# Expert search by fetched rows: indirect transfers of the chosen rows of both tables in place of dense products with all 16384 of them

## The chip, the cores and the metric

The program runs on one core of a Trainium2 chip as one launch. The metric is the device time of that launch in microseconds. TensorE is called PE here, VectorE DVE, ScalarE ACT, GpSimd POOL and SyncE SP, as in the profile.

## The reference, cut to what matters

Three blocks follow each other on 256 tokens of width 1024: a recurrent and attention block with a feed-forward part, a block with two kinds of attention and an expert search, and a block with long convolutions and 16 experts. The change touches the expert search of the second block and the vectors that modulate the second and third block.

```python
mod = jax.nn.silu(c) @ ada_w[l] + ada_b[l]             # six vectors; the third block has six more
...
def peer(h, wq, subkeys, u_tab, v_tab):                # h 256 x 1024; the tables 16384 x 1024
    q = (hf @ wq).reshape(T, PEER_HEADS, 2, PEER_DKEY // 2)
    sc = jnp.einsum('thpd,pnd->thpn', q, subkeys, preferred_element_type=jnp.float32)
    top_v, top_i = lax.top_k(sc, PEER_TOPK)            # 16 of 128, twice for each of 8 heads
    cand_v = (top_v[:, :, 0, :, None] + top_v[:, :, 1, None, :]).reshape(T, PEER_HEADS, -1)
    cand_id = (top_i[:, :, 0, :, None] * PEER_NKEYS + top_i[:, :, 1, None, :]).reshape(T, PEER_HEADS, -1)
    best_v, best_j = lax.top_k(cand_v, PEER_TOPK)      # 16 of 256 sums
    ids = jnp.take_along_axis(cand_id, best_j, axis=-1)
    ...                                                # g = softmax of best_v, by heads
    def block(args):
        xb, ib, gb = args
        ub = jnp.take(u_tab, ib, axis=0)
        a = jnp.einsum('td,ted->te', xb, ub, preferred_element_type=jnp.float32)
        w = gb * jax.nn.gelu(a, approximate=False)
        vb = jnp.take(v_tab, ib, axis=0)
        return jnp.einsum('te,ted->td', w.astype(vb.dtype), vb)
```

So each token has 8 x 16 = 128 chosen rows of either table.

## The kernel before

All weights come as one stream of 128 x 1024 pieces (512 KB) through a ring of five buffers that SP fills (K.start, K._load, L82 to L95). A product asks for its next piece by K.get (L114): ACT rounds the piece to an upper part whi (L108), DVE subtracts for a lower part wlo (L112), and up to three pieces are split ahead. A product of float32 accuracy is then three PE instructions (mm3, L155, with the lines L158 to L160). Some pieces of the stream are not taken by a product but consumed where they come: those of the modulation vectors (K.modulation, L329), eight pieces for each of twelve vectors. DVE multiplies such a piece by a column of silu(c) and adds it to a sum (L362 for the first, L364 for the others); four small products with ones and one DVE addition then make the vector (total, L343). The lists plan1 (L374), plan2 (L771) and plan3 (L1312) set the order of the stream: 32 of the 96 modulation pieces stand in the first block's feed-forward part, 8 in the second block's attention, 24 in the pass over the first table, 32 in the one over the second.

The function peer (L1028) is the expert search. Eight pairs of pieces of wq give the queries (L1064), four float32 products for each head give the scores of the half keys (L1072). What DVE does to choose runs as small background steps between the weights: top16 (L1082) on 128 scores twice and on 256 sums once, for 8 heads and 2 halves of the tokens, then gate (L1105) and decode (L1114). The chosen pairs go to DRAM by POOL's queue (pick_parts, L1142).

Nothing waits for the choice at first: the first table is multiplied whole. 128 pieces of peer_u give the products of all 16384 rows with all tokens, gelu of which fills A, four tiles of 32 KB a partition (gelu, L1170, over 64 pairs). Then the gates are spread over A: for four tokens at a time PE works out distances (L1198, L1199), ACT and DVE make one-hot operands of them (L1205, L1206), PE multiplies these (L1224) and DVE multiplies A by the result (L1231). No weights are used in that time. Then the second table is multiplied whole as well: 128 pieces of peer_v, each with 12 products of 128 x 128 by 128 x 512 (the loop after prep, L1249), into four banks, with the parts of A as the other operand (L268, L269).

From the middle of the second table's pass on, the spectra of the third block's filters are worked out in small steps between the weights (Spectra.steps, L1396); the products of the last three of eight pieces are held back until the second table is done, and lie beside the update of x (L1294, L1295) and the start of the third block (block3, whose first DVE addition is L1534). From there to the end nothing of the change is met again: the third block's products, and its 16 experts, whose weights come in pieces of 512 KB and of 1 MB (L1809).

Of the kernel before, what the change touches and what calls it, by code (L numbers as in the profile page):

```python
# [22 lines left out]
S = 256  # L23
# [4 lines left out]
# columns of the packed per-partition vectors: name -> (first column, count)  # L28
# [11 lines left out]
class K:  # L40
    """Pools, constants and the helpers that every part uses."""
# [4 lines left out]
    def __init__(self, ctx, tc, a):  # L46
# [14 lines left out]
        self.sums = None  # L61
# [35 lines left out]
    def _process(self, wait=False, lower=None):  # L97
        """Split the next item, or have it consumed; the lower part later, by what this returns, where wait is set."""
# [15 lines left out]
    def get(self):  # L114
        """The upper and the lower part of the next weights."""
# [13 lines left out]
    def ahead(self, n):  # L129
        """Have the parts of n weights ready; the look ahead goes on."""  # L130
# [4 lines left out]
    def drain_raw(self):  # L135
        """Consume the raw items that come next."""
# [25 lines left out]
    def cols_of(self, hT, out):  # L162
        """out [128 n, 256 t] = the next 1024 x 128 weights^T hT."""
# [4 lines left out]
    def pair(self, hT):  # L168
        """[128 n, 2, 256 t] of the next two tiles."""
# [5 lines left out]
    def rows_part(self, ps, hT, q, n=8):  # L175
        """Two banks [128 t, 512 n] (+)= a quarter of hT^T the next 256 x 512 weights, summed by n tiles."""
# [7 lines left out]
    def rows_of(self, hT, after=None):  # L184
        """Two banks [128 t, 512 n] = hT^T the next 1024 x 512 weights; after(q) follows each quarter of them."""
# [32 lines left out]
    def rms(self, pool, x, name, n=1024, junk=None):  # L218
        """1/rms of the rows of x [128, 2, n] -> [128, 2]."""
# [10 lines left out]
    def square(self, t, h, junk):  # L230
        """The sums of squares over half h of the rows t of x, for rms_x."""
# [2062 lines left out]
```

## Time and profile before

| what | us |
|---|---|
| device time, three runs without profile: median (lowest to highest) | 2697.01 (2696.55 to 2697.32) |
| span of the profiled execution, first to last instruction | 2692.9 |
| busy in it: PE, DVE, ACT, POOL | 2375.5, 1423.8, 881.2, 81.0 |
| its mean granted PE clock, of full speed | 0.924 |

The time of the profiled execution itself is not listed beside its span; the median of the other runs lies 4.1 us above the span. PE is busy for 88% of the span, but that is an average over stages: the profile's slices show PE at 9 tenths and more from the start to about 1700 us and at 7 tenths afterwards, with the DMA engines at 9 tenths and more from about 1800 us on. Stages are told apart by what runs in them: the first block to 462 us, the second block's attention to 623, the queries to 681, the first table to 1050, the gates to 1145, the second table to 1534, the third block to about 1750, the experts to the end.

### The profile page before, as it was taken

The numbers are of one execution on the slowest core, as the hardware profiler recorded it, in microseconds if no ns is written. First come the engines' busy times: TensorE is split into PE (matmuls) and PEld (weight loads), VectorE is DVE, ScalarE is ACT, GpSimd is POOL, SyncE is SP. The second block draws the span as 40 slices with busy tenths as digits, with TensorE's granted clock in tenths as the row PEclk, the third lists the DMA queues.
The fourth block names the chain that finished last, engine by engine and source line by source line (L and its number), as shares of the span: only waits on it lengthen the run. The fifth ranks groups of instructions, "written<-read, shape, count | busy, mean of one in ns | idle before, by whom it ended". The sixth has DMA issues, their size and how long they took to land.

```text
span 2692.9 us, 38200 instructions
## 1 busy us (share of the span) xinstructions
PE 2375.5 (88%) x15289; PEld 1722.5 (64%) x15289; DVE 1423.8 (53%) x2416; ACT 881.2 (33%) x1263; POOL 81.0 (3%) x65
## 2 busy tenths in 40 slices
PE   9999999999999999999999999787766666767676
PEld 8899998889999998777788899431211221211222
DVE  7876887767888866877777888610000000000001
ACT  5764544564444444444455544200000000000000
POOL 0100000000000000000000013100000000000000
PEclk9999999999999999999999999788777878877787
DMA  6555787744566775078855634899999999999997
GB/s 218 166 158 170 250 283 244 233 136 136 174 185 182 244 262 171 4 245 284 290 172 172 180 118 163 327 357 415 414 416 416 414 416 415 414 414 415 416 414 306
DMA packets 189481, 727.75 MB, mean 270 GB/s; under 512 B 31258, under 2 KB 36471, under 8 KB 165239
## 3 DMA queue, kind: packets, MB, share of 16 engines
q1 hardware_dynamic: 176086, 712.72, 72.5%
q10 hardware_dynamic: 13120, 12.32, 1.5%
q8 instruction: 120, 1.97, 0.3%
q14 instruction: 59, 0.48, 0.1%
q0 software_dynamic: 96, 0.26, 0.0%
HBM read 723.88 MB, written 1.36 MB: 269 GB/s over the span
## 4 chain that ended last, share of the span: by engine, by line
PE 62%; DMA 30%; DVE 5%; ACT 1%; issue 1%; POOL 0%; SPq 0%; POOLq 0%; ACTq 0%; DVEq 0%
DMA K<-in_moe_w_dram 14%; PE mm L158 11%; PE mm L160 11%; PE mm L159 11%; DMA we<-in_moe_w_dram 10%; DMA wraw<-in_moe_w_dram 5%; PE ac L158 5%; PE ac L160 5%; PE ac L159 5%; PE gated L1224 3%; PE mm L1973 1%; PE mm L2034 1%; DVE wlo L112 1%; PE mm L1930 1%; PE dist L1198 1%
## 5 line engine op out<-in xcount | busy, mean ns | idle before, releaser
L112 DVE TENSOR_TENSOR wlo<-wraw,whi 128x1024 fp32r<-128x1024 f32 x479 | 586.9, 1228 | 281.6 <-ACT whi L108 278.7
L108 ACT ACTIVATE whi<-wraw 128x1024 fp32r<-128x1024 f32 x484 | 510.9, 1059 | 562.7 <-PE mm L159 241.1
L158 PE MATMUL mm<-hT3h,whi 128*128 128x256 f32 x1152 | 327.6, 284 | 0.0
L1932 DVE TENSOR_TENSOR xe<-mm,m 128x256 f32<-128x256 f32 x15 | 6.4, 425 | 606.6 <-PE mm L1930 606.6
L159 PE MATMUL mm<-hT3l,whi 128*128 128x256 f32 x1152 | 326.7, 284 | 0.0
L160 PE MATMUL mm<-hT3h,wlo 128*128 128x256 f32 x1152 | 326.4, 283 | 0.0
L158 PEld LDWEIGHTS mm<-hT3h,whi 128*128 128x128 f32 x1152 | 221.6, 192 | 1.3 <-issue 1.2
L1973 PE MATMUL mm<-K,xe 128*32 128x512 f32 x864 | 150.3, 680 | 81.7 <-DMA K<-in_moe_w_dram 81.7
L159 PEld LDWEIGHTS mm<-hT3l,whi 128*128 128x128 f32 x1152 | 221.5, 192 | 0.4 <-DVE hT3l L316 0.4
L160 PEld LDWEIGHTS mm<-hT3h,wlo 128*128 128x128 f32 x1152 | 221.5, 192 | 0.0
L1973 PE MATMUL mm<-we,xe 128*32 128x512 f32 x864 | 148.3, 781 | 82.0 <-DMA we<-in_moe_w_dram 81.6
L158 PE MATMUL ac<-whi,Wh 128*128 128x512 f32 x512 | 204.9, 400 | 0.0
L160 PE MATMUL ac<-whi,Wl 128*128 128x512 f32 x512 | 202.2, 395 | 0.1
L159 PE MATMUL ac<-wlo,Wh 128*128 128x512 f32 x512 | 202.0, 394 | 0.0
L158 PE MATMUL mm<-hTh,whi 128*128 128x256 f32 x608 | 171.4, 282 | 0.8 <-DVE hTl L301 0.8
L160 PE MATMUL mm<-hTh,wlo 128*128 128x256 f32 x608 | 169.3, 278 | 2.8 <-DVE wlo L112 2.8
L159 PE MATMUL mm<-hTl,whi 128*128 128x256 f32 x608 | 168.9, 278 | 0.0
L1973 PEld LDWEIGHTS mm<-K,xe 128*32 128x32 f32 x864 | 22.1, 114 | 201.8 <-DMA K<-in_moe_w_dram 188.0
L1973 PEld LDWEIGHTS mm<-we,xe 128*32 128x32 f32 x864 | 21.0, 121 | 201.5 <-DMA we<-in_moe_w_dram 180.4
L2013 ACT ACTIVATE he<-mm 128x512 f32<-128x512 f32 x16 | 9.5, 596 | 417.7 <-PE mm L1973 417.7
L2022 ACT ACTIVATE heT<-mm 128x512 f32<-128x512 f32 x16 | 9.6, 597 | 383.2 <-PE mm L2020 383.2
L2040 DVE TENSOR_TENSOR ye<-mm,m 128x512 f32<-128x512 f32 x16 | 11.1, 692 | 212.9 <-PE mm L2034 212.9
(535 smaller groups left out, 4578.0 us busy)
## 6 DMA issues: line engine op xcount, KB each, us to landing
we<-in_moe_w_dram SPq DMA_DIRECT2D x160, 1024.0 KB
K<-in_moe_w_dram SPq DMA_DIRECT2D x122, 1024.0 KB
wraw<-in_peer_u_dram SPq DMA_DIRECT2D x128, 512.0 KB
wraw<-in_peer_v_dram SPq DMA_DIRECT2D x128, 512.0 KB
wraw<-in_moe_w_dram SPq DMA_DIRECT2D x100, 512.0 KB
K<-in_moe_w_dram SPq DMA_DIRECT2D x84, 512.0 KB
wraw<-in_w_in_dram SPq DMA_DIRECT2D x48, 512.0 KB
wraw<-in_ada_w_dram SPq DMA_DIRECT2D x48, 512.0 KB
```

The costliest lines, as they stand in the source:

```text
L108: nc.scalar.activation(hi, raw, AF.Copy)
L112: (lower or nc.vector).tensor_sub(lo, raw, hi)
L158: nc.tensor.matmul(out, lhs[0], rhs[0], start=start, stop=False)
L159: nc.tensor.matmul(out, lhs[0], rhs[1], start=False, stop=False)
L160: nc.tensor.matmul(out, lhs[1], rhs[0], start=False, stop=stop)
L1198: nc.tensor.matmul(p, z[0:14], mv[0:14], start=True, stop=True)
L1224: nc.tensor.matmul(p[:, g % 2 * 4 + i], o[0][:, i], o[1][:, i], start=True, stop=True)
L1930: nc.tensor.matmul(p[:, c], hl[:, t, c * 128:c * 128 + 128], oh[:, t, e], start=t == 0, stop=t == 1)
L1973: nc.tensor.matmul(p[32 * j:32 * j + 32], xe[:, c], w[j], start=c == 0, stop=c == 7)
L2022: nc.scalar.activation(heT, p, AF.Copy)
L2034: nc.tensor.matmul(p[32 * g:32 * g + 32], heT[:, o:o + 32], w[2 * fh + dh], start=q == 0, stop=q == 7)
L2040: nc.vector.tensor_mul(ye, p, m5)
```

## The change

The two dense passes, the one-hot products and the round trip of the chosen pairs through DRAM are gone. The tables are laid side by side in DRAM as one table uv of 16384 rows of 8 KB, a row of peer_u and the same row of peer_v behind it. A list s is one head for one half of the tokens (16 lists, 16 choices each); a choice e of a list is one item n = 16 s + e, and an item is one indirect transfer from POOL's queue that brings 128 rows, one for each token of the half, each to its token's partition: 128 x 2048 numbers, 1 MB. There are 256 items.

For each item DVE multiplies the u half of the rows by the tokens' h2 (held in PSUM, tokens on the partitions) and sums along the row (dot); ACT takes gelu of two sums at a time; DVE makes a diagonal matrix of the result times the gate (weigh); PE multiplies the v half of the rows by that diagonal, two float32 products of 128 x 128 by 128 x 512, and sums over the items in PSUM (add). Items go two by two in batches; the diagonals and products of a batch are issued in the next one, between its two dots. A place of 1 MB is freed by an item's products and refilled at once. There are 12 places at first, 17 from the end of the queries' products on, when the split buffers are given up, and 9 after batch 52, when two tiles are closed for the third block's filters.

Choosing is cut into 13 DVE steps for each list: the first list is chosen whole before the first transfer, three steps go before each of the six batches that lie between the queries' products, two after each of the others. The filters' spectra go one step a batch from about batch 58 on (the 67 steps come in two halves, the second from about batch 97 on, two steps a batch), and none of their products is held back. All 96 modulation pieces now stand in the first two blocks: 40 before the feed-forward part, 40 in it, 16 in the second block's attention.

```diff
         def use(s, ch):
             def f(raw):
                 if ch == 0:
-                    assert state.get("s", s) == s
-                    state["a"] = self.sums.tile([128, 1024], F32, name="mod_a", bufs=1)
-                    state["b"] = self.sums.tile([128, 256], F32, name="mod_b", bufs=1)
+                    if len(state) == self.sums_bufs:
+                        total(s - len(state))
+                    state[s] = [self.sums.tile([128, n], F32, name=f"mod_{n}", bufs=self.sums_bufs)
...
+def spread(weights, raw, first=0):
+    p, n, m = [], 0, len(weights) - first
+    for i, z in enumerate(weights):
+        p.append((z, None))
+        while i >= first and n < len(raw) * (i - first + 1) // m:
+            p.append(raw[n])
+            n += 1
...
+    return spread(p, early, 6) + spread(f, late, 8)
...
-    m = mod3 + late
-    for j in range(128):
-        p.append((a['peer_u'][j], None))
...
-    for j in range(128):
-        p.append((a['peer_v'][:, j], None))
...
+    return spread(p, raw, 2) + [(z, None) for z in o]
...
+    def refill():
+        while places and st['n'] < N and (st['n'] // 16 in ids):
+            owner, z = places.pop(0)
...
+            i = ids[n // 16]
+            nc.gpsimd.indirect_dma_start(out=z, out_offset=None, in_=a['uv'], in_offset=bass.IndirectOffsetOnAxis(ap=i[:, n % 16:n % 16 + 1], axis=0))
...
+    def dot(n):
+        u = rows[n][1][:, 0:1024]
+        nc.vector.scalar_tensor_tensor(u, u, 1.0, h2[0], op0=ALU.mult, op1=ALU.mult, accum_out=dots[s][:, e:e + 1])
...
+    def gelu(n):
+        nc.scalar.activation(acts[s][:, e:e + 2], dots[s][:, e:e + 2], AF.Gelu)
...
+    def weigh():
+        for n in pend:
+            d = tk.tile([128, 128], F32, name='diag', bufs=4)
+            nc.vector.tensor_scalar(d, k.ident, acts[s][:, e:e + 1], gates[s][:, e:e + 1], op0=ALU.mult, op1=ALU.mult)
...
+    def add(r):
+        for n, d in r:
+            for j in range(2):
+                nc.tensor.matmul(ys[0][:, 512 * j:512 * j + 512], d, rows[n][1][:, 1024 + 512 * j:1536 + 512 * j], start=n % 128 == 0, stop=n % 128 == 127)
+            release(n)
+        refill()
...
+    def batch(b):
+        n = 2 * b
+        dot(n)
+        r = weigh()
+        dot(n + 1)
+        gelu(n)
+        add(r)
+        if b == 64:
+            finish(0)
+        pend[:] = [n, n + 1]
...
     for r in range(8):
         k.later(half_scores, r, k.pair(hT))
+        if r == 1:
+            pump(99, 0)
+            refill()
+        if r >= 2:
+            pump(3, 1)
+            batch(nb)
+            nb += 1
+            refill()
...
-    for j2 in range(64):
-        k.later(gelu, j2, k.pair(hT))
...
+    for b in range(nb, N // 2):
+        if b == 64:
+            tokens(1)
+        batch(b)
+        pump(2, st['n'] // 16 + 3)
+        refill()
+        if b == 52:
+            closed.update(('E0', 'G0'))
...
+        for _ in range(1 if b < 96 else 2):
+            k.settle()
+            if steps:
+                steps.pop(0)()
```

Three places show what the engines are given. On DVE, in the stretch where the chosen indices are worked out, the order before is this (wlo are the lower parts of the first table's pieces, early is the tile that holds the scores and lists):

```order
L112 TENSOR_TENSOR wlo<-wraw,whi 128x1024
L1125 TENSOR_TENSOR early<-early,iota_6514 128x512
L1129 TENSOR_TENSOR early<-early 128x512
L1130 TENSOR_REDUCE early<-early 128x32
L112 TENSOR_TENSOR wlo<-wraw,whi 128x1024 x2
```

And this is a piece of the order now, a batch and the first half of the next (rowsL and rowsS are places, h is h2, dots the sums, diag the diagonals):

```order
L1200 SCALAR_TENSOR_TENSOR rowsL,dots<-rowsL,h_6944 128x1024
L1090 MAX early<-early 128x8
L1091 MAX_INDEX early<-early 128x8
L1093 MATCH_REPLACE early<-early 128x128
L1090 MAX early<-early 128x8
L1091 MAX_INDEX early<-early 128x8
L1200 SCALAR_TENSOR_TENSOR rowsL,dots<-rowsL,h_6944 128x1024
L1216 TENSOR_SCALAR diag<-ident,acts,gate 128x128 x2
L1200 SCALAR_TENSOR_TENSOR rowsS,dots<-rowsS,h_6944 128x1024
```

The lower parts of weights are gone from DVE; two dots and two diagonals a batch take their place, and the steps of choosing stand behind the batch's second dot, so that a dot that waits for its rows holds them up.

On PE, this is the order before at the end of the first table and the start of the gates (hT3 are the parts of h2, pk the chosen pairs):

```order
L158 MATMUL mm<-hT3h,whi 128x256
L159 MATMUL mm<-hT3l,whi 128x256
L160 MATMUL mm<-hT3h,wlo 128x256
L1198 LDWEIGHTS pk_7245
L1198 MATMUL dist_11625<-ohm,pk_7245 128x512
```

And now, in the later part of the fetched rows, where the filters' spectra run beside them (ys is the sum over the items, KR the transform's matrix and the filters' parts):

```order
L1226 MATMUL ys<-G_6765,diag 128x512 x2
L1226 MATMUL ys<-rowsL,diag 128x512 x4
L1226 MATMUL ys<-rowsS,diag 128x512 x2
L158 MATMUL mm<-KR 128x256
L159 MATMUL mm<-KR 128x256
L160 MATMUL mm<-KR 128x256
```

PE's long runs of products with weights become four float32 products a batch, and each spectrum step's products wait behind the batch's.

On POOL's queue this stood in the same part of the program before:

```order
L112 TENSOR_TENSOR wlo<-wraw,whi 128x1024
L1152 MEMSET pk_7245 37x512
L1142 DMA picks<-early 128x4x128 x2
L1211 MEMSET pk_11618 37x512
L1525 MEMSET px_router 128x256
```

And now (early, G and G are the first twelve places):

```order
L112 TENSOR_TENSOR wlo<-wraw,whi 128x1024
L1174 DMA early_6762<-in_uv_dram,ids 128x2048 x3
L1174 DMA G_6763<-in_uv_dram,ids 128x2048 x4
L1174 DMA G_6765<-in_uv_dram,ids 128x2048 x4
L1174 DMA early_6762<-in_uv_dram,ids 128x2048 x4
L1174 DMA G_6763<-in_uv_dram,ids 128x2048 x4
```

POOL, which issued two transfers in the whole program, issues 256, in the order of the items, each waiting for its place and its list.

## Rows read from the trace of the kernel before

**Rows 1.** Stretches of the span, by stage: start and end in us, their length, then the busy us (and instructions) of PE, PEld, DVE, ACT and POOL, the granted PE clock, the DMA engines' share and GB/s.

```profile
0.00:275.00 275.00, 262.76 (x1807) 242.97 (x1808) 200.88 (x353) 158.02 (x249) 15.46 (x10) 0.99 0.57 176
275.00:462.00 187.00, 185.37 (x1340) 170.00 (x1339) 155.70 (x192) 87.38 (x100) 0.00 (x0) 1.00 0.81 273
462.00:623.00 161.00, 154.08 (x977) 131.44 (x975) 116.39 (x226) 88.97 (x188) 12.99 (x9) 0.97 0.53 168
623.00:681.00 58.00, 57.20 (x469) 56.67 (x469) 41.98 (x110) 29.58 (x49) 0.00 (x0) 0.98 0.51 152
681.00:1050.00 369.00, 369.00 (x3083) 367.11 (x3082) 288.95 (x546) 172.34 (x199) 1.91 (x3) 1.00 0.68 218
1050.00:1145.00 95.00, 93.74 (x649) 71.38 (x646) 83.15 (x191) 44.39 (x66) 0.35 (x1) 1.00 0.04 9
1145.00:1534.00 389.00, 388.94 (x1788) 312.63 (x1787) 296.91 (x340) 192.60 (x235) 0.00 (x0) 1.00 0.68 227
1750.00:2650.00 900.00, 646.02 (x3636) 187.98 (x3628) 55.14 (x103) 21.07 (x36) 0.00 (x0) 0.81 1.01 411
```

**Rows 2.** The chain that ended last, cut to 600 to 1760 us, shares by line.

```profile
by line: PE mm L160 15.0%; PE mm L158 14.9%; PE mm L159 14.9%; PE ac L158 10.4%; PE ac L160 10.3%; PE ac L159 10.2%; PE gated L1224 5.9%; PE dist L1198 1.7%; PE mm L1973 1.7%; issue 0.9%; PE mm L1429 0.7%; PE mm L1944 0.7%; PE mm L1072 0.6%
```

**Rows 3.** The timeline at the start of the queries and at the end of the second table: start and length in us, engine, line, operation.

```profile
622.67 0.58 PE L158 MATMUL mm<-hT3h,whi 128*128 128x256 f32 x1
...
1533.71 0.69 DVE L1294 TENSOR_TENSOR K<-ac,g 128x512 f32<-128x512 f32 x1 [1.66 <-PE ac L160]
1534.44 0.69 DVE L1295 TENSOR_TENSOR x<-x,K 128x512 f32<-128x512 f32 x1
...
1539.31 1.78 DVE L1534 TENSOR_TENSOR x<-x,K 128x512 f32<-128x512 f32 x1
```

**Rows 4.** DVE instructions of the forms that a batch will have, by their lines: count, shortest, median and longest in ns, first and last start.

```profile
L1538 DVE SCALAR_TENSOR_TENSOR x<-x,rsf,K x2: 1277/1281/1285, 1544.8 to 1546.2; 128x1024 f32<-128x1024 f32 x2
L1538 DVE DVE_READ_ACCUMULATOR x<-x,rsf,K x2: 82/83/84, 1546.0 to 1547.4; 128x1 f32 x2
L1119 DVE TENSOR_SCALAR early<-early x2: 220/220/221, 834.1 to 885.6; 128x128 uint32<-128x128 uint32 x2
```

**Rows 5.** Instructions on the tile early (the choice) from 626.5 to 1050 us, and on the tile K (the filters' spectra) from 1145 to 1534 us, columns as in rows 1.

```profile
626.50:1050.00 423.50, 8.91 (x66) 8.06 (x66) 136.67 (x474) 10.55 (x26) 1.74 (x2) 1.00 0.66 210
```
```profile
1145.00:1534.00 389.00, 13.87 (x80) 8.67 (x80) 72.64 (x111) 28.61 (x45) 0.00 (x0) 1.00 0.68 227
```

**Rows 6.** Float32 products on PE: by line as in rows 4, at 128 and at 512 columns, and one piece of the experts' timeline.

```profile
L1224 PE MATMUL gated<-oh,oh x512: 275/275/377, 1051.4 to 1143.9; 128*128 128x128 f32 x171
```
```profile
L1999 PE MATMUL ac<-x,ident x8: 592/1061/1061, 1771.1 to 1776.3; 128*128 128x512 f32 x8
```
```profile
1802.61 3.62 PE L1973 MATMUL mm<-we,xe 128*32 128x512 f32 x32
```

**Rows 7.** Transfers: two issue lines of the page, and two stretches as in rows 1.

```profile
we<-in_moe_w_dram SPq DMA_DIRECT2D x160, 1024.0 KB
wraw<-in_peer_u_dram SPq DMA_DIRECT2D x128, 512.0 KB
```
```profile
380.00:400.00 20.00, 20.00 (x147) 18.79 (x146) 17.70 (x24) 9.79 (x12) 0.00 (x0) 1.00 0.90 324
...
1800.00:2600.00 800.00, 566.29 (x3182) 158.84 (x3174) 40.98 (x78) 15.53 (x26) 0.00 (x0) 0.82 1.02 415
```

**Rows 8.** The transfers that POOL issues: their instruction as in rows 4, and the time from issue to landing in us.

```profile
L1142 POOL DMA_DIRECT2D picks<-early x2: 768/872/976, 878.3 to 931.2; - x2
...
DMA to landing us min/median/max: 4.3/4.6/4.9
```

**Rows 9.** The timeline where POOL computes beside DVE, and the same DVE form without POOL (by line, as in rows 4).

```profile
615.44 2.34 POOL L112 TENSOR_TENSOR wlo<-wraw,whi 128x1024 fp32r<-128x1024 f32 x1 [3.48 <-ACT whi L108]
615.53 3.91 DVE L1059 TENSOR_SCALAR early<-x,rsm 128x1024 f32<-128x1024 f32 x2
```
```profile
L834 DVE TENSOR_SCALAR on<-x,rsm x2: 748/748/749, 467.1 to 467.8; 128x1024 f32<-128x1024 f32 x2
```

**Rows 10.** The modulation sums on DVE by line, as in rows 4, and the three fullest stretches of DVE before the feed-forward part, as in rows 1.

```profile
L364 DVE SCALAR_TENSOR_TENSOR mod_a<-wraw,mod_t,mod_a x84: 1274/1279/1283, 279.8 to 1332.3; 128x1024 f32<-128x1024 f32 x84
```
```profile
20.00:40.00 20.00, 20.00 (x113) 17.40 (x112) 17.81 (x47) 10.62 (x15) 0.00 (x0) 1.00 0.62 193
100.00:120.00 20.00, 19.90 (x133) 17.93 (x131) 18.43 (x20) 17.66 (x24) 4.70 (x2) 1.00 0.54 169
120.00:140.00 20.00, 18.10 (x153) 17.57 (x154) 19.28 (x31) 10.18 (x14) 0.00 (x0) 1.00 0.52 154
```

More of the change, by code (lines that the diff above doesn't have):

```diff
@@ L279, in transposed, with full @@
         nc = self.nc
+        def full(n, c):
+            return tmp[n] if isinstance(tmp, list) else tmp[:, c]
         hi, lo = hT
@@ new lines, in peer, with pump, add_places, views @@
+    work = [(s, f) for s in range(16) for f in choose(s)]
+    def pump(n, upto):
+        while n and work and work[0][0] <= upto:
+            work.pop(0)[1]()
+            n -= 1
+    N = 256
+    places, rows, use = [], {}, {}
+    def add_places(owner, tiles):
+        use[owner] = 0
+        places.extend((owner, z) for z in tiles)
+    def views(tile):
+        return [tile[:, 2048 * i:2048 * i + 2048] for i in range(4)]
+    add_places("E0", views(E0)[1:])
+    add_places("G0", views(G0))
@@ new lines, in peer @@
+    add_places("G1", views(G1))
+    places.append(("E0", views(E0)[0]))
+    closed = set()
+    st = {"n": 0}
+    def refill():
+        while places and st["n"] < N and st["n"] // 16 in ids:
+            owner, z = places.pop(0)
+            if owner in closed:
+                continue
+            n = st["n"]
+            z = z() if callable(z) else z
+            rows[n] = owner, z
+            use[owner] += 1
+            i = ids[n // 16]
+            nc.gpsimd.indirect_dma_start(out=z, out_offset=None, in_=a["uv"],
+                                         in_offset=bass.IndirectOffsetOnAxis(ap=i[:, n % 16:n % 16 + 1], axis=0))
+            st["n"] += 1
@@ new lines, in release, with tokens @@
+    def release(n):
+        owner, z = rows.pop(n)
+        use[owner] -= 1
+        if owner not in closed:
+            places.append((owner, again.get(owner, z)))
+    again = {}
+    h2 = [None]
+    def tokens(t):
+        h2[0] = ps.tile([128, 1024], F32, name="h2")
+        for c in range(8):
+            nc.tensor.transpose(h2[0][:, c * 128:c * 128 + 128], hfull[:, c, t * 128:t * 128 + 128], k.ident)
+    dots, acts, pend = {}, {}, []
+    def dot(n):
+        s, e = n // 16, n % 16
+        if e == 0:
+            dots[s] = tk.tile([128, 16], F32, name="dots", bufs=3)
+        u = rows[n][1][:, 0:1024]
+        nc.vector.scalar_tensor_tensor(u, u, 1.0, h2[0], op0=ALU.mult, op1=ALU.mult, accum_out=dots[s][:, e:e + 1])
@@ L1210, in peer @@
[L1210 to L1234 removed]
+    assert not k.parts
@@ L1236, in peer @@
+    add(weigh())
+    k.settle()
+    while steps:
+        steps.pop(0)()
+        k.settle()
+    F.loads()
+    finish(1)
+    k.settle()
     ps.release()
+    pr.release()
+    pl.release()
+    tk.release()
     k.ps = tc.alloc_tile_pool(name="ps2", bufs=4, space=PSUM, reuse_waits="tile")
[L1238 to L1244 removed]
@@ L1389, in constant, with steps @@
         return [lambda i=i: self.k.parts_of(parts[0][:, i], parts[1][:, i], r[:, i]) for i in range(n)]
-    def space(self, pool):
-        self.room = [self.R[:, 7168:8192]] + [pool.tile([128, 1024], F32R, name=f"held{i}") for i in range(3)]
-        return pool
-    def steps(self):
+    def steps(self, o):
         k, N = self.k, 256
@@ L1417, in split @@
         def split(o, ch, s):
-            if o and ch in (1, 2):
-                z = self.room[2 * (ch - 1) + s]
-                return [z[:, 512 * i:512 * i + 512].rearrange("p (t c) -> p t c", t=2) for i in range(2)]
             b = 5120 + 1024 * s
@@ L1544, in block3 @@
     k.still = False
-    for f in F.held[4:]:
-        f()
     k.settle()
```

415 lines of the change are left out of this document (148 added, 267 removed).

## The prediction

> **What bounds the kernel now.** I read the stages first [rows 1]: a share of the whole span says little here, since the stages have different limits. Through both blocks and the whole expert search PE is the full engine: 369 of 369 us in the first table, 94 of 95 in the gates, 389 of 389 in the second table, at a granted clock of 1.00. DVE is second there with 76 to 88% and the DMA engines move 218 and 227 GB/s, and next to nothing during the gates. In the experts it is the other way round: the DMA engines are full at 411 GB/s and PE waits. The chain says the same of the stretch in question: the weights' products have three quarters of it, the gates' products 8% [rows 2]. So what is taken from PE between 681 and 1534 us is taken from the end, if nothing else fills that time; and the experts' stretch, which hangs on its own bytes, follows unchanged.
>
> The stretch that the change rewrites runs from the first product of the queries at 622.7 us to the first addition of the third block at 1539.3, when x is complete [rows 3]: 916.6 us.
>
> **What replaces it.** Four resources have to be priced for a batch of two items.
>
> *Fetching.* An item is 1 MB in rows of 8 KB. The nearest row is the experts' 1 MB pieces, which stream at 415 GB/s for 800 us [rows 7]: 1.049 MB / 415 = 2.53 us an item, 5.05 a batch. The 512 KB pieces of 4 KB rows give a second rate: 324 GB/s at a share of 0.90, so 360 when full, 2.91 us an item. Rows picked at random are like neither; I take the first, since size of transfer and of row are the same, and keep the second for the range. The Trainium skill (DMA: Bandwidth & Descriptors, Where 436 GB/s comes from) holds that a load from DRAM is bound by about 358 GB/s a core; by that figure an item would take 2.93 us and the sum below would end at 2593; the experts' 415 GB/s speak against it as a limit of this core.
>
> *DVE.* A dot is the form of L1538 with its accumulator read: 1.281 + 0.083 = 1.364 us; a diagonal is a 128-column tensor_scalar, 0.220 [rows 4]. Two of each make 3.17 us a batch. Choosing costs 136.7 us for 16 lists [rows 5], 8.5 a list; seven short instructions that served a half of the tokens are now issued for each list, so I take 9.5 a list, 1.46 for two of 13 steps. The spectra cost DVE 72.6 us [rows 5], 1.1 us for each of 67 steps.
>
> *PE.* A float32 product is two instructions in the rows (512 for 256 products on L1224). Their lengths, 275 ns at 128 columns and 592 at 512, differ by 0.83 ns a column, so 512 columns occupy PE for 0.42 us, and eight passes of four column groups take 3.62 us, 0.43 each [rows 6]. A batch is four products, eight passes: 3.45 us at full clock. At the lower of PE's two levels, 1.2 GHz, an instruction takes 1061 ns, 0.47 longer than at 2.4 GHz [rows 6], so about 0.86 to 0.9 a pass, 6.9 us or more a batch.
>
> *POOL.* An indirect transfer is in no row. Below stands the instruction of the plain transfers, 0.87 us for 512 pieces of 256 B; above, their 4.6 us from issue to landing, as if each transfer had to land before the next is begun [rows 8]. With eight or more places waiting I take it near the lower end, under 2.5 us, so that fetching sets the pace.
>
> Now the stages. **Queries with the first six batches:** 58 us as before [rows 1], plus the products of five batches, 5 x 3.45 = 17, plus eight transposes of h2, 2 us, plus 3 us in which DVE waits for the first rows (10 us of choosing, then a transfer of about 5, against three pieces split ahead): 80 us. The first list is chosen beside products that are under way. **Batches 6 to 57:** DVE 3.17 + 1.46 = 4.63, PE 3.45, fetching 5.05, which wins: 52 x 5.05 = 263. **Batches 58 to 96,** where a spectrum step joins the choice: DVE 3.17 + 1.46 + 1.10 = 5.73 is now above fetching; 39 x 5.73 = 224. **Batches 97 to 113,** choice done, two steps each: 3.17 + 2.20 = 5.37; 17 x 5.37 = 91. **Batches 114 to 127:** fetching, 14 x 5.05 = 71. The queue of filled places (12, later 9) lets fetching and DVE catch up with each other between these parts; against that gain stand the turn between the token halves at batch 64, where DVE waits for transposes and PE for the update of x, and late lists. I leave both out of the sum. **End:** the last four products 3.5 and the second half's update, four DVE instructions of 0.69 as L1294 and L1295 [rows 3], 2.8: 6. Sum 80 + 263 + 224 + 91 + 71 + 6 = 735 us against 916.6: **182 us less**.
>
> **The modulation pieces.** In the two tables they cost PE nothing, so taking 56 of them away gains nothing that is not counted. In the first two blocks each adds 1.28 us of DVE [rows 10]: 40 before the feed-forward part make 51 us on top of 201 in 275, eight more there 10 on 156 in 187, eight more in the attention 10 on 116 in 161 [rows 1]. On average PE covers it. Where DVE is fullest it does not: 3.9 us more for every 20 us puts 17.8, 18.4 and 19.3 at 21.7, 22.3 and 23.2 [rows 10], an excess of 7 us that PE waits for; with the order on DVE, where a piece stands ahead of the next weights' lower part, I take 12 us, from 0 to 35. The DMA share of 0.57 there has room for 21 MB.
>
> The third block's held-back products go, but they only lie beside a chain of DVE and ACT steps; I cost them at nothing, up to 5 us more or less. Nothing later changes, so a shift of the third block's start shifts the end.
>
> Sum: -182 + 12 = -170. The profiled span of 2692.9 becomes 2523; with the 4.1 us that the median of the runs lies above it, **2527 us**.
>
> **Rivals.**
>
> *Rows come more slowly than pieces.* For: they are scattered, and half-size pieces move at 360 GB/s. Against: every row is 8 KB. At 2.91 us an item a batch takes 5.82 in all four parts, 122 x 5.82 = 710 instead of 649: 2588 us.
>
> *POOL cannot issue fast enough, and the kernel gets slower.* Place: POOL's queue, where 234 transfers are still to be made ready after the queries. The gain of 170 is spent when a batch takes (649 + 170) / 122 = 6.71 us, 3.36 us an item; at 4.6 an item [rows 8] the batches take 1122 us and the kernel 3000. For: the program has no indirect transfer to show, and POOL and DVE get into each other's way in this trace: two DVE instructions of L1059 took 3.91 us together beside a POOL instruction of 2.34, where two of the same form on L834 take 0.75 each [rows 9], and DVE would be busy nearly without a break. Against: 512 pieces took POOL 0.87 us, an item has 128. The Trainium skill (SBUF — State Buffer, SBUF: two separate sides) has the rule that speaks against this change: POOL writes the descriptors of its transfers through a port pair that it shares with DVE, and a DVE instruction in a two-port mode shuts it out until it ends. By that rule the short diagonals and copies would hold POOL up, some 0.5 us a batch, and not the dots.
>
> *The clock.* In the experts PE is busy for 0.72 of the stretch, waits for each piece, and is granted 0.81 [rows 1]. If it stood at the lower level through all batches, 122 x 6.9 = 842 instead of 649: 2720 us, slower. Against: at that level PE would never wait, and the three stretches from 681 to 1534 us, in which PE hardly waits, are granted 1.00.
>
> *A full overlap.* If places in stock even out fetching and DVE, 234 items and some 6 MB of the filters' tables beside them take 606 us, and the blocks cover all their sums: 43 + 12 us less, 2472.
>
> **How the numbers follow.** Chances: forecast 0.50 (2490 to 2560), slower rows 0.24, POOL 0.15, the clock 0.03, full overlap 0.08. What a measurement of this kernel can tell from no change is 0.2%, 5 us. The range must hold 8 in 10: forecast, overlap and slower rows make 0.82, so it goes from 2470 to 2660, which is a batch of 6.3 us. Faster: 0.50 + 0.24 + 0.08, and a little of a mild POOL, 0.83; the same 0.02; slower 0.15.
>
> **What would show it.** Right: the stretch from the queries to the third block takes about 735 us; DMA at 0.95 and 400 GB/s or more in batches 6 to 57, then DVE above 0.95 with dots of 1.36 us; PE near 0.7 with a clock of 0.95 or more; POOL's instruction under 2.5 us; the first block longer by about 10 us and PE there waiting for wlo. Wrong: DVE waiting for rows while the DMA engines are not full (POOL), DMA full at 360 GB/s (slow rows), PE full at a clock near 0.5, or PE in the first block waiting for more than 35 us.

## The result: 118 us less, where 170 were forecast

| what | before | now |
|---|---|---|
| device time, median of the runs shown with this result (lowest to highest) | 2696.78 (2696.3 to 2697.32) | 2578.41 (2575.36 to 2579.39) |
| ratio, 95% interval | | 0.9556 (0.9543 to 0.957) |
| span of the profiled execution | 2692.9 | 2577.2 |
| its mean granted PE clock | 0.924 | 0.898 |

The forecast was 2527 us with a range of 2470 to 2660: the direction and the range held, and the time came out 51 us above the forecast. First the places that answer to [rows 3], from the timeline of the changed kernel: start and length in us, engine, line, operation.

```profile
651.77 0.58 PE L158 MATMUL mm<-hT3h,whi 128*128 128x256 f32 x1
...
1419.47 1.51 DVE L1531 TENSOR_TENSOR x<-x,K 128x512 f32<-128x512 f32 x1
```

The first product of the queries comes 29.1 us later than before (622.67), so the two first blocks lost that much. From there to the first DVE addition of the third block it now takes 767.7 us, against 916.6: 148.9 less. From that addition to the end it is 1157.7 us against 1153.6, 4.1 more. 29.1 - 148.9 + 4.1 = -115.7, which is the difference of the spans.

The stretch in between is cut at the starts of the dots that open batches 0, 6, 58, 97 and 114. These are the windows of the changed kernel as in [rows 1]: both first blocks; the queries with the first six batches; batches 6 to 57; 58 to 96; 97 to 113; 114 to 127; and the experts.

```profile
0.00:651.80 651.80, 614.21 (x4175) 548.59 (x4175) 537.89 (x831) 333.46 (x535) 29.40 (x18) 0.98 0.72 241
651.80:734.60 82.80, 68.10 (x431) 57.76 (x430) 54.39 (x131) 29.81 (x54) 20.23 (x20) 0.88 0.80 314
734.60:992.10 257.50, 206.07 (x485) 85.20 (x484) 219.06 (x602) 36.20 (x90) 98.53 (x105) 0.98 1.01 416
992.10:1212.90 220.80, 170.79 (x449) 77.68 (x449) 197.93 (x503) 41.61 (x90) 74.32 (x76) 0.92 0.96 381
1212.90:1345.70 132.80, 96.50 (x299) 49.41 (x297) 85.31 (x164) 18.48 (x45) 34.67 (x36) 0.86 0.85 326
1345.70:1410.90 65.20, 54.17 (x139) 24.39 (x140) 41.31 (x85) 4.14 (x17) 19.64 (x21) 0.97 0.87 349
1600.00:2500.00 900.00, 638.02 (x3568) 189.56 (x3564) 69.66 (x161) 23.53 (x41) 2.38 (x2) 0.81 1.00 406
```

| part | forecast, us | measured, us |
|---|---|---|
| first two blocks, more than before | 12 (0 to 35) | 29.1 |
| queries and first six batches | 80 | 82.8 |
| batches 6 to 57 | 263 | 257.5 |
| batches 58 to 96 | 224 | 220.8 |
| **batches 97 to 113** | **91** | **132.8** |
| batches 114 to 127 | 71 | 65.2 |
| end | 6 | 8.6 |
| third block to the end, more than before | 0 (-5 to 5) | 4.1 |

Two lines carry the error: 42 us in seventeen batches and 17 us in the first two blocks; the other lines give 5 us back in sum. That makes 54 us on the spans; it is 51 on the medians, since the median now lies 1.2 us above the profiled span and not 4.1. In batches 6 to 57 the DMA engines are full at 416 GB/s, as forecast. In 97 to 113 nothing is full: DMA 0.85, DVE 85 of 133 us, PE 97.

The instructions of a batch by their lines, as in [rows 4] and [rows 8]:

```profile
L1200 DVE SCALAR_TENSOR_TENSOR G<-G,h x120: 1200/1215/1223, 694.6 to 1409.6; 128x1024 f32<-128x1024 f32 x120
L1200 DVE DVE_READ_ACCUMULATOR G<-G,h x120: 70/83/85, 695.7 to 1410.8; 128x1 f32 x120
...
L1216 DVE TENSOR_SCALAR diag<-ident,acts,gate x256: 327/343/578, 694.1 to 1411.4; 128x128 f32<-128x128 f32 x128
...
L1174 POOL DMA_INDIRECT G<-in_uv_dram,ids x120: 935/939/1765, 679.5 to 1396.2; - x120
```

A dot takes 1.30 us (forecast 1.36), a diagonal 0.34 (0.22), an indirect transfer holds POOL for 0.94 (0.87 to 4.6). Now what DVE waited for in batches 97 to 113, and then what PE waited for: us in total, times, longest.

```profile
DVE KR L269 <- ACT KR L268: 17.8, 6, 7.1
DVE K L142 <- PE mm L1441: 17.3, 4, 4.5
DVE K L142 <- PE mm L1424: 5.9, 2, 3.7
DVE K L1433 <- ACT K L1430: 4.7, 4, 1.2
DVE rowsL L1200 <- DMA rowsL<-in_uv_dram,ids: 0.7, 1, 0.7
```
```profile
PE ys L1226 <- DVE diag L1216: 33.8, 11, 6.8
```

DVE's waits are 46 us, 2.7 a batch, and nearly all stand inside the spectrum steps; rows are waited for once. PE's 34 us are all for diagonals. A piece of the timeline there shows how they come about (in brackets the idle time ahead of an instruction, and what ended it):

```profile
1227.47 0.68 DVE L1436 TENSOR_TENSOR K<-K 128x512 f32<-128x512 f32 x1
1228.18 0.69 DVE L1437 TENSOR_TENSOR K<-K 128x512 f32<-128x512 f32 x1
...
1229.93 0.60 DVE L1216 TENSOR_SCALAR diag<-ident,acts,gate 128x128 f32<-128x128 f32 x2
1230.33 5.74 PE L1226 MATMUL ys<-rowsL,diag 128*128 128x512 f32 x8 [6.75 <-DVE diag L1216]
...
1238.05 0.59 PE L1441 MATMUL mm<-K,ones 128*128 128x256 f32 x2
...
1238.68 1.76 DVE L142 RECIPROCAL K<-mm 128x256 f32<-128x256 f32 x1 [4.22 <-PE mm L1441]
```

PE stands for 6.75 us until DVE, busy and waiting in a spectrum step (K), comes to the diagonals. Then PE has the items' products and a step's products first, the small product of L1441 comes last, and DVE stands for 4.22 us until it is there. In that time DVE makes no diagonals for the next batch. Each engine goes through its own queue in order, and each stands while the other has work for it further back.

### The profile page after: what moved, and what is told of

Same layout as the page of the kernel before. It is cut to its first block, busy times and chain, and to the rows that moved or that the text cites. A ratio compares the mean times of both kernels' runs of the same rounds, so it can differ in the third digit from the quotient of the medians.

```text
span 2577.2 us, 29437 instructions
## 1 busy us (share of the span) xinstructions
PE 2063.1 (80%) x11067; PEld 1200.5 (47%) x11067; DVE 1374.0 (53%) x2774; ACT 566.4 (22%) x998; POOL 326.8 (13%) x317
## 3 DMA queue, kind: packets, MB, share of 16 engines
q0 software_dynamic: 36864, 268.45, 25.8%
## 5 line engine op out<-in xcount | busy, mean ns | idle before, releaser
L112 DVE TENSOR_TENSOR wlo<-wraw,whi 128x1024 fp32r<-128x1024 f32 x223 | 276.2, 1242 | 95.9 <-ACT whi L108 94.1
L108 ACT ACTIVATE whi<-wraw 128x1024 fp32r<-128x1024 f32 x228 | 239.5, 1056 | 177.9 <-PE mm L159 53.1
L1226 PE MATMUL ys<-G,diag 128*128 128x512 f32 x480 | 228.9, 617 | 50.7 <-DVE diag L1216 50.5
L1200 DVE SCALAR_TENSOR_TENSOR G<-G,h 128x1024 f32<-128x1024 f32 x120 | 145.5, 1214 | 25.7 <-DMA G<-in_uv_dram,ids 25.3
L1226 PE MATMUL ys<-rowsS,diag 128*128 128x512 f32 x252 | 126.3, 641 | 36.3 <-DVE diag L1216 29.5
L1174 POOL DMA_INDIRECT G<-in_uv_dram,ids x120 | 115.4, 962 | 207.2 <-PE ys L1226 100.7
L1226 PE MATMUL ys<-rowsL,diag 128*128 128x512 f32 x168 | 96.5, 716 | 49.0 <-DVE diag L1216 48.6
L158 PEld LDWEIGHTS mm<-hTh,whi 128*128 128x128 f32 x608 | 115.4, 190 | 4.8 <-issue 2.0
L159 PEld LDWEIGHTS mm<-hTl,whi 128*128 128x128 f32 x608 | 116.2, 191 | 0.7
L160 PEld LDWEIGHTS mm<-hTh,wlo 128*128 128x128 f32 x608 | 115.3, 190 | 0.4 <-DVE wlo L112 0.2
```

Of the source, the lines that this page charges most:

```text
L108: nc.scalar.activation(hi, raw, AF.Copy)
L112: (lower or nc.vector).tensor_sub(lo, raw, hi)
L158: nc.tensor.matmul(out, lhs[0], rhs[0], start=start, stop=False)
L159: nc.tensor.matmul(out, lhs[0], rhs[1], start=False, stop=False)
L160: nc.tensor.matmul(out, lhs[1], rhs[0], start=False, stop=stop)
L1174: nc.gpsimd.indirect_dma_start(out=z, out_offset=None, in_=a["uv"], in_offset=bass.IndirectOffsetOnAxis(ap=i[:, n % 16:n % 16 + 1], axis=0))
```

## Experiments

All are edits of the changed kernel but `sums_alone`. Ratios are to the kernel before; the changed kernel has 0.9556 (0.9543 to 0.957).

### The spectrum steps: what holds batches 97 to 113

**step_between.** One of the two steps stands between the dots.

```diff
     def batch(b, mid=None):
         dot(n)
         r = weigh()
+        if mid:
+            mid()
         dot(n + 1)
...
-        batch(b)
+        batch(b, one if b >= 96 else None)
...
-        for _ in range(1 if b < 96 else 2):
-            k.settle()
-            if steps:
-                steps.pop(0)()
+        one()
```

> The changed kernel, with the second spectrum step of batches 96 to 127 put between the batch's two dots, where it stood right behind the first one. Theory: these batches are long (7.8 us each, 97 to 113) since DVE waits for PE and ACT inside two steps in a row, 46 us in all; with a dot between two steps most of it is covered: 2578 less 25 to 40, 2538 to 2553 us. Rival, that the work itself is what takes the time (DVE, or PE at its lower clock): within 5 us of 2578.

Measured: 2545.09 us, ratio 0.9438 (0.9423 to 0.9452), 33 us less than the changed kernel. Batches 97 to 113 in windows, and DVE's largest waits in them:

```profile
1211.10:1313.30 102.20, 86.79 (x298) 45.37 (x298) 83.73 (x161) 16.43 (x41) 35.53 (x36) 0.97 1.01 409
```
```profile
DVE K L142 <- PE mm L1446: 5.6, 2, 2.9
DVE K L1438 <- ACT K L1435: 4.7, 4, 1.2
DVE KR L269 <- ACT KR L268: 3.7, 4, 1.3
```

132.8 became 102.2 us with the same work (DVE 84 us against 85), the waits shrank from 46 to 18 us, and the DMA engines are full again. PE's waits for diagonals fell from 34 to 15 us. So it was waiting and not DVE's work. PE's granted clock rose from 0.86 to 0.97 with it, and PE was busy for 10 us less with as many instructions; no run here tells how much of the 31 us came by way of the clock. The other parts moved by 2 us or less each.

**steps_behind.** No step beside the batches.

```diff
         for _ in range(1 if b < 96 else 2):
             k.settle()
-            if steps:
-                steps.pop(0)()
     add(weigh())
```

> The changed kernel with all spectrum steps behind the last batch and none beside the batches. Theory: batches 58 to 127 fall to the fetching rate, about 5.0 us, 69 us less in all; the steps by themselves then take their DVE work of 72 us and at least the 57 us that DVE waits in them now: 2578 - 69 + 130 = 2639 us or more. Rival, that only the steps' work counts and no waits between engines: 2578 - 69 + 73 = 2582 us.

Measured: 2609.75 us, ratio 0.9671 (0.9657 to 0.9686): between the two. Windows of batches 64 to 96, 97 to 113, and of the end with all the steps:

```profile
1026.10:1195.90 169.80, 125.17 (x264) 49.06 (x264) 140.25 (x380) 22.98 (x57) 62.87 (x67) 0.97 1.01 415
1195.90:1284.00 88.10, 62.66 (x133) 24.50 (x134) 52.24 (x108) 3.46 (x17) 31.05 (x34) 0.98 1.01 421
1352.30:1452.70 100.40, 68.04 (x344) 54.88 (x343) 74.44 (x115) 32.56 (x57) 0.00 (x0) 0.80 0.12 39
```

Without steps, fetching bounds the batches, 5.15 and 5.18 us each, as both theories had it. But the steps by themselves take about 92 us (100.4 less the 8.6 of the end), some 20 more than DVE's 72: my 57 us of waits don't belong to the steps alone. The rest comes with the batches; by the piece of timeline above, from the items' products, which stand on PE between two halves of a step, and from the diagonals that those wait for.

**diag_on_act.** The diagonals leave DVE.

```diff
-            nc.vector.tensor_scalar(d, k.ident, acts[s][:, e:e + 1], gates[s][:, e:e + 1], op0=ALU.mult, op1=ALU.mult)
+            w = acts[s][:, e:e + 1]
+            nc.scalar.activation(w, w, AF.Copy, scale=gates[s][:, e:e + 1])
+            nc.scalar.activation(d, k.ident, AF.Copy, scale=w)
```

> The changed kernel with the diagonals made by ACT (the activation times the gate, then the identity times that) in place of DVE. Theory: batches 6 to 57 are bound by fetching and stay at 4.83 and 5.08 us; batches 64 to 96 are bound by DVE, are freed of 0.69 us each and fall from 5.75 to about 5.1 us, 21 us less; 97 to 113 lose up to 12 us: 2578 less 21 to 33, 2545 to 2557 us. Rival, that the time from dots to diagonals sets the pace or that the chain through ACT is longer: 2573 us or more.

Measured: 2522.51 us, ratio 0.9352 (0.9336 to 0.9368), 56 us less than the changed kernel and more than I expected. Windows of batches 32 to 57, 64 to 96, 97 to 113:

```profile
855.60:986.80 131.20, 97.00 (x209) 38.17 (x210) 97.00 (x248) 50.08 (x147) 48.81 (x52) 0.99 1.01 421
1018.80:1191.90 173.10, 144.02 (x395) 67.03 (x394) 155.73 (x369) 76.76 (x212) 63.82 (x66) 0.94 1.01 410
1191.90:1292.00 100.10, 84.59 (x298) 45.03 (x296) 77.20 (x130) 38.47 (x113) 33.53 (x35) 0.97 1.02 418
```

Batches 32 to 57 stay (131.2 against 132.0 us), as they must where fetching is the bound, though DVE has 13 us less to do. Batches 64 to 96 fall from 189.6 to 173.1, somewhat less than expected, and 97 to 113 by 32.7 us where I had given them up to 12: with the diagonals on another queue PE's waits for them fall from 34 to 15 us, and DVE's waits from 46 to 22. That breaks the same knot at its other end. Some 6 us come from the first six batches. PE's waits in batches 97 to 113 now:

```profile
PE ys L1228 <- ACT diag L1218: 15.4, 8, 3.5
```

**between_and_act.** Both edits.

> Both edits together, the second spectrum step between the dots and the diagonals on ACT. Theory: what each takes off stands in other batches, so that the gains add up: 2545 us of the first edit less 21 in batches 64 to 96 and about 10 in 97 to 113, 2514 us (2508 to 2526). Rival, that fetching or PE takes over at once: 2540 us or more.

Measured: 2519.65 us, ratio 0.934 (0.9326 to 0.9354). The total lies in the expected range: behind the first edit the second still takes 16 us out of batches 64 to 96, where 21 were expected, and 6.5 out of 97 to 113, where 10 were. But the gains as measured apart, 33 and 56 us, do not add up: together they are 59. In batches 97 to 113 it is 30.6 and 32.7 us apart, 37.1 together (95.7 us). Both remove one wait, and behind it fetching is the bound:

```profile
1190.00:1285.70 95.70, 85.59 (x290) 44.45 (x289) 75.91 (x126) 36.27 (x106) 34.16 (x35) 0.96 1.02 418
```

This is the fastest kernel here, 177 us below the kernel before and 59 below the change; its interval overlaps that of the diagonals on ACT alone.

### Fetching: rows picked at random, their length, and POOL

**rows_in_line.** The same bytes from neighbouring rows.

```diff
-            nc.gpsimd.indirect_dma_start(out=z, out_offset=None, in_=a["uv"],
-                                         in_offset=bass.IndirectOffsetOnAxis(ap=i[:, n % 16:n % 16 + 1], axis=0))
+            nc.gpsimd.dma_start(out=z, in_=a["uv"][n % 128 * 128:n % 128 * 128 + 128])
```

> The changed kernel with each indirect transfer replaced by a plain one on the same queue that brings 128 neighbouring rows of the table, so the fetched rows are not the chosen ones. Theory: rows picked at random come as fast as neighbouring ones, and batches 6 to 57 stay at 4.95 us: 2578 us within 6. Rival, that scattered rows or POOL's work on them slow the fetching: batches at 4.8 us and less with more than 430 GB/s, 2568 us or less.

Measured: 2567.84 us, ratio 0.9521 (0.9506 to 0.9535). By the time alone the rival has it. Batches 6 to 57 say otherwise:

```profile
727.20:984.50 257.30, 207.53 (x486) 85.80 (x484) 218.43 (x602) 36.20 (x90) 55.41 (x105) 0.97 1.00 412
```

257.3 against 257.5 us: scattered rows of 8 KB cost nothing, though POOL has only 55 us to do in place of 99. The 11 us come from elsewhere: 7 before batch 6, where plain transfers need no list (the first dot starts at 678.7 instead of 682.2 us; why the first six batches are 4 us shorter is not shown), and 3 in batches 97 to 113. My expectation had no bound for that; the time of a part decided, not the total.

**two_tables.** Two transfers of 4 KB rows for an item.

```diff
-            nc.gpsimd.indirect_dma_start(out=z, out_offset=None, in_=a["uv"],
+            for m, tab in enumerate((a["u"], a["v"])):
+                nc.gpsimd.indirect_dma_start(out=z[:, 1024 * m:1024 * m + 1024], out_offset=None, in_=tab,
```

> The changed kernel with the two tables apart: an item is two indirect transfers of 128 rows of 4 KB in place of one of 8 KB, with the same bytes. Theory of size: rows of 4 KB come at 360 GB/s as the pieces of half the size did, so batches 6 to 57 take 5.82 us, 50 us more in all: 2628 us. Rival, that the row's length doesn't matter and POOL has time for twice as many transfers (4 of 0.94 us a batch, 3.8 of 5.1): 2578 us within 6.

Measured: 2663.32 us, ratio 0.9874 (0.9859 to 0.9889), 85 us more than the change. Windows of batches 6 to 31 and 32 to 57:

```profile
741.50:912.20 170.70, 114.84 (x276) 49.68 (x275) 107.92 (x302) 18.94 (x48) 108.29 (x116) 0.88 0.92 352
912.20:1056.00 143.80, 104.11 (x212) 41.71 (x210) 106.69 (x301) 17.15 (x42) 97.53 (x102) 0.89 0.97 371
```

In 32 to 57 an item comes in 2.77 us, 379 GB/s, against 2.54 in the changed kernel (132.0 us): with the DMA engines nearly full (0.97) a shorter row does cost, less than the 360 GB/s of [rows 7] say. Batches 6 to 31 took 45 us longer though the DMA engines were not full there, and that no theory of mine had. Their timeline, DVE first and then POOL:

```profile
772.38 0.16 DVE L1114 TENSOR_SCALAR early<-early 128x16 uint32<-128x16 uint32 x1
776.38 0.18 DVE L1115 CAST early<-early 128x32 f32<-128x32 uint32 x1 [3.83 <-remote]
777.78 0.69 DVE L1118 TENSOR_TENSOR early<-early,iota 128x512 f32<-128x512 f32 x1 [1.22 <-issue]
778.38 1.21 DVE L1201 SCALAR_TENSOR_TENSOR rowsL<-rowsL,h 128x1024 f32<-128x1024 f32 x1
```
```profile
773.39 0.94 POOL L1175 DMA_INDIRECT early<-in_v_dram,ids  x1 [0.31 <-issue]
774.64 0.94 POOL L1175 DMA_INDIRECT early<-in_u_dram,ids  x1 [0.30 <-issue]
775.88 0.94 POOL L1175 DMA_INDIRECT early<-in_v_dram,ids  x1 [0.30 <-issue]
```

While POOL issues transfers back to back, short DVE instructions stand for microseconds, and the trace names no engine of this program as their releaser; dots in between run at their usual 1.21 us. The Trainium skill (SBUF — State Buffer, SBUF: two separate sides) has DVE and POOL share a port pair: whichever starts first holds it for its whole instruction, and the other is blocked. These rows point the same way, with DVE as the loser, where I had priced POOL; but a wait of 3.83 us is longer than the 0.94 us of one POOL instruction, so that rule alone does not give it. No run here separates the port pair from another cause, so it stays open.

### The modulation pieces in the first two blocks

**sums_alone.** The kernel before with nothing but this move.

```diff
-    k.start(plan1(a, items2[:32]) + plan2(a, items2[32:40], items2[40:], items3) + plan3(a))
+    raw = items2 + items3
+    k.start(plan1(a, raw[:40], raw[40:80]) + plan2(a, raw[80:]) + plan3(a))
```

> The kernel before with nothing but the move of the modulation pieces (40 before the feed-forward part, 40 in it, 16 in the second block's attention, none in the tables). Theory: the move alone makes the first two blocks 29 us longer, as they are in the changed kernel, and the tables, where PE is full, give back only the 4 us or so of the vectors' small products: 2697 + 25 = 2722 us (2717 to 2727). Rival, as forecast: 12 us, 2709. Rival, that the 29 us come from something else in the change: 2697 or less.

Measured: 2719.88 us, ratio 1.0083 (1.0069 to 1.0097), 23 us more. A second run for its trace:

> The kernel before with the move of the modulation pieces alone, once more, for its trace. Theory: the first query product starts 29 us later than in the kernel before (651.8 against 622.7 us), 16 us of it by the last of the first block's gate projections, and the tables then take 5 us less, for the vectors' products that PE no longer does there: first addition of the third block at 1539 + 24 = 1563 us. Rival, that the tables give back more and the blocks lose more, or that the loss stands elsewhere: a first query product outside 649 to 655 us.

```profile
650.74 0.58 PE L158 MATMUL mm<-hT3h,whi 128*128 128x256 f32 x1
```

2719.69 us; the blocks end 28.1 us later and the third block starts 22.5 us later, so the tables gave back 5.6. The move costs by itself what it costs in the changed kernel.

Where? The starts of the weights' products can be paired one by one between the kernel before and the changed one, since their order is the same. The lag is 0.5 us at 60 us, 7.4 at 120, 16.3 at 136, 14.3 at 140 (the kernel before has a wait of its own there), 16.0 at 200, 19.6 at 477 (the end of the first block's feed-forward part), 24.2 at 504 and 29.1 at 651.8. The largest piece, 9 us of which 7 stay, is one event. First PE at its end, then DVE, then POOL:

```profile
129.77 1.08 PE L355 MATMUL mm<-mod,ones 128*32 128x256 f32 x8 [5.45 <-DVE mod L372]
```
```profile
120.89 1.27 DVE L577 TENSOR_TENSOR_SCAN om<-aa,xa 128x256 f32<-128x256 f32 x2
122.08 2.85 DVE L112 TENSOR_TENSOR wlo<-wraw,whi 128x1024 fp32r<-128x1024 f32 x1
124.85 2.38 DVE L575 TENSOR_TENSOR xa<-xa,om 128x512 f32<-128x512 f32 x1
127.26 1.27 DVE L577 TENSOR_TENSOR_SCAN om<-aa,xa 128x256 f32<-128x256 f32 x2
128.45 1.26 DVE L372 SCALAR_TENSOR_TENSOR mod<-wraw,mod_t,mod 128x1024 f32<-128x1024 f32 x1
```
```profile
121.66 5.02 POOL L533 TENSOR_TENSOR qkT<-qk 128x1024 f32<-128x1024 f32 x2 [27.74 <-PE mm L160]
```

Beside two POOL products, 5.02 us together, two DVE instructions take 2.85 and 2.38 us where the same forms take 1.22 and 0.69 at 119 to 121 us; the scans and a vector's last sum come late, and PE stands for 5.45 us before that vector's small products. From then on the granted clock is at its lower level, 1.2 GHz, for 6.6 us, as this window shows (columns as in [rows 1]); that is where most of the rest of the 9 us went.

```profile
128.60:135.20 6.60, 5.43 (x28) 4.63 (x29) 6.57 (x8) 0.41 (x1) 0.00 (x0) 0.50 0.56 169
```

The kernel before has the same two POOL products, 4.70 us from 114.28 us on, and DVE is as slow beside them: 2.38 us where 0.69 is usual, and 2.85 for two scans that usually take 1.27. There PE waits for 1.37 us only. First DVE, then PE:

```profile
114.84 2.38 DVE L561 TENSOR_TENSOR xa<-xa,om 128x512 f32<-128x512 f32 x1
117.26 2.85 DVE L563 TENSOR_TENSOR_SCAN om<-aa,xa 128x256 f32<-128x256 f32 x2
```
```profile
121.28 0.39 PE L160 MATMUL mm<-hTh,wlo 128*128 128x256 f32 x1 [1.37 <-DVE wlo L112]
```

So the slow stretch beside POOL is not new; new is that DVE, with the modulation sums in its queue, has no idle time left to make up for it. `first_sums_out` below bears this out: without these sums the lag does not jump here.

**sums_later.** These products three pieces further back.

```diff
-                    self.later(self.later, total, s)
+                    self.later(self.later, self.later, self.later, self.later, self.later, total, s)
```

> The changed kernel with each modulation vector's four small products put three pieces of weights further back on PE. Theory: the largest single loss of the first two blocks is PE's wait of 5.5 us for one such vector's last sum, with the fall of the clock for 6.8 us behind it: 2578 less 9, 2569 us (2566 to 2572). Rival, that DVE is late there anyway, so that PE waits for the next lower part instead: 2578 us within 4.

Measured: 2574.39 us, ratio 0.9546 (0.9533 to 0.9559): 4 us less, at the rival's bound, with intervals that overlap. The wait of 5.5 us is gone, PE waits 3.6 and 1.1 us for lower parts there instead, and the lag at the products of 140 us is 11.6 us where it was 14.3; but at those of 210 us it is 18.0 where it was 16.0. DVE is what is late; the order behind it matters little.

**sums_left_out, first_sums_out, all_sums_out.** Pieces loaded and dropped; the diff is that of the first, the second has `which == 3` there and the third `False`.

```diff
-                else:
+                elif which == 2:
                     z = state[s][0]
                     nc.vector.scalar_tensor_tensor(z, raw, th[:, ch:ch + 1], z, op0=ALU.mult, op1=ALU.add)
```

> The changed kernel without 42 of the 56 added modulation sums: of each of the third block's six vectors only the first piece is used, the other seven are loaded and dropped, so these vectors are incomplete. Loads, ring and the vectors' products stay. Theory: DVE's time in the first two blocks is what the move costs, so that most of the 29 us goes in proportion: 2578 less 42/56 of 24 (29 without the 5 of the vectors' products on PE), 2560 us (2555 to 2564). Rival, that the added 512 KB pieces in the ring or the vectors' products on PE cost the time: 2574 us or more.

Measured: 2570.4 us, ratio 0.9528 (0.9509 to 0.9547), 8 us less: neither. I had mistaken where these pieces stand. The 40 ahead of the feed-forward part are the second block's, and their sums were all still there; the lag was still 15 us by the place where it is 16.3, and 25.8 at the queries.

> The changed kernel without the modulation sums of the second block's six vectors beyond each one's first piece: 42 pieces are loaded and dropped, 35 of them before the feed-forward part, where 16 of the 29 us are lost (the run before left sums out behind that stretch only). The second block's vectors are incomplete, so other rows are fetched. Theory: DVE's work on these pieces is what costs the 16 us; PE is held up by less than 4 us there: 2578 less 12 to 16, 2562 to 2566 us. Rival, that loading 40 pieces through the ring is the cost: the 16 us stay, 2574 us or more.

Measured: 2566.52 us, ratio 0.9513 (0.9497 to 0.9528), 12 us less. The lag by the same place is 2 us instead of 16, at the products of 200 us 5 instead of 16, and 16.3 at the queries.

> The changed kernel with only the first piece of each of the twelve modulation vectors used, 84 pieces loaded and dropped. Theory: the gains of the two runs before add up, 7 and 12 to 16 us: 2578 less 19 to 23, 2555 to 2559 us, and what is left of the 29 us is loads and the vectors' products on PE. Rival: 2570 us or more.

Measured: 2558.11 us, ratio 0.9481 (0.9465 to 0.9497), 20 us less, as expected. The lag at the queries is 12.9 us. So 16 of the 29 us go with DVE's 84 additions. The kernel before makes 35 of these in the two blocks as well, but there PE waits for lower parts for only 3.8 us in all, so that most of the 16 belong to the 49 that the move added. Of the rest, some 5 are the products of seven more vectors on PE, by their busy time (that form takes 8.1 us in the two blocks, 3.2 before); 8 stay open, with the loads and the seven vectors' first pieces on DVE (0.75 us each) among the candidates.

## Why the prediction was right, and by how much it was not

**What bounds, and that taking PE's tables away shortens the end: right.** 148.9 us went out of the stretch of 916.6.

**Fetching: right.** 4.95 us a batch against 5.05. The rate of the experts' pieces was the right row, and random order cost nothing. The Trainium skill's 358 GB/s (DMA: Bandwidth & Descriptors, Where 436 GB/s comes from) does not bound this core here: the rows came at 416 GB/s.

**DVE: right in sum, in part by luck.** Dots were 5% cheaper, diagonals 0.12 us dearer; batches 58 to 96 came out at 5.66 us each against 5.73. But DVE's work there was 5.08 us a batch, 0.65 less than priced, and waits made up for it: DVE was at 0.90, not above 0.95.

**PE: harmless.** PE was at 0.80 in batches 6 to 57, 3.96 us a batch where 3.45 were priced, and still under fetching.

**Batches 97 to 113: the step that failed.** I wrote DVE 3.17 + 2.20 = 5.37 us, "choice done, two steps each", that is, work with no waits. The work was even less, 85.3 / 17 = 5.02 us; the waits came on top, 2.7 us a batch, and a batch took 7.8. A step's own round trips between DVE, PE and ACT lay beside the second table before, where PE was busy for 388.94 of 389 us [rows 1] and so did not wait for DVE; with diagonals in the same queue they meet PE's need of DVE. The places in stock could not help, since it was not rows that were missing. That late lists and turns were left out of the sum did no harm; the waits inside the steps should have stood there.

**The modulation: right in kind, mis-sized.** 12 us forecast, 29.1 measured, inside the bounds of 0 to 35. I had counted three full stretches by their mean excess; that DVE is slow beside POOL (the 4.70 us of POOL stand in [rows 10]) and has no idle time left to make up for it, and the seven more vectors' products on PE, had no term. PE waited 6.2 us in the two blocks for vectors' last sums, which I had not named; for wlo, which I had, it waited 6.2 us as well, but 3.8 of these were there before.

**Third block: inside its 5 us,** at the unfavourable end; why is not shown.

**The rivals.** The total, 2578, lies outside the band of 2490 to 2560 that I gave the forecast, and near the 2588 of the slower rows. By the total alone that rival would have won; by the parts it fell, with rows at 416 GB/s. The range held by luck: it reached so far up for the sake of slower rows, which did not come, and not for waits inside steps, which did. (Its upper end, 2660, is a batch of 6.4 us and not of 6.3.) POOL fell by a wide margin: 0.94 us an item against a break-even of 3.36; its stands were waits for free places. The clock did not stay low: 0.98 in batches 6 to 57 and 0.86 in 97 to 113. The full overlap did not come, but `between_and_act` takes away 59 us of what stood in its way.

## What to carry to other kernels

Adding up an engine's instruction times prices a stretch only if nothing in its queue waits; before moving a chain of round trips next to a loop, ask which instructions of the loop stand behind it in the same queue, and give these to an engine whose queue the chain holds up less (ACT here, which has a part in the steps too, so that 15 us of PE's waits were left). Two edits that undo the same wait don't add up. And a total that lands on a rival's number can come from another part: cut the time by parts before believing it.

## What was not expected of the hardware

- An indirect transfer of 128 rows held POOL for 0.94 us with rows of 8 KB; with 4 KB rows it was the same 0.94, with 0.30 us between two, so half the row is twice POOL's work for the same bytes.
- Scattered rows of 8 KB moved at 416 to 421 GB/s with full DMA engines, as fast as neighbouring ones (412); rows of 4 KB at 379.
- With 573 instructions on POOL in place of 317, short DVE instructions stood for up to 7.9 us while POOL issued; why is not shown. In the change itself no wait of this kind shows. Where DVE made two lower parts there beside a transfer (2.35 us, as long as without one), it was the transfer that held POOL for 2.19 us in place of 0.94.
